# RWKV keys stage: the decay's small-rank products issued one key tile sooner than the rate's

## The chip, the cores and the metric

The kernel runs on one core of one Trainium2 chip. The metric is the time of one execution on the device in microseconds (us); several executions are timed and the median is given. One more execution is recorded by the hardware profiler, and all rows shown come from such a record. The engines are TensorE (PE in the rows; its weight loads are PEld), VectorE (DVE), ScalarE (ACT), GpSimd (POOL) and SyncE (SP), whose queue issues nearly all DMA transfers here.

## What is computed

The program is one inference step of a two-layer trunk on 1104 token rows: 8 sample sequences of 8 tokens, then a prompt of 16 + 1024. Layer 0 is a gated DeltaNet mixer, layer 1 an RWKV-7 mixer. Only the projections at the start of layer 1 matter here:

```python
xs = xn[None] + xx[None] * mu[:, None, None, :]             # six token-shifted mixes of the input
rkvz = jnp.einsum('sbtd,sde->sbte', xs[:4], w_rkvz)         # four 1024 x 1024 projections
r, k, v, z = rkvz[0], rkvz[1], rkvz[2], rkvz[3]
w = -jax.nn.softplus(-(w0 + jnp.tanh(xs[4] @ w1) @ w2)) - 0.5     # decay: rank 64
a = jax.nn.sigmoid(a0 + (xs[5] @ a1) @ a2)                        # rate: rank 64
kk = l2norm((k * k_k).reshape(B, T, H, N))
k = k * (1.0 + (a - 1.0) * k_a)
decay = jnp.exp(-jnp.exp(w))
```

The decay does not use the keys. The second form of the keys, `k * (1 + (a - 1) * k_a)`, needs keys and rate of the same columns.

## The kernel before, in words

All activations lie transposed: 128 features on the partitions, tokens along the free dimension, in three segments of 384, 384 and 336 tokens (`SEGS`). A 1024-wide result is made of 8 tiles of 128 features; in the keys projection they are called key tiles 0 to 7. A float32 product is made of three matmuls on rounded halves (high times high, high times low, low times high), so one segment of a key tile takes 8 x 3 = 24 matmuls and a whole key tile 72.

The keys stage is `keys_decay_rate` (L1425). It first prepares `w2`, the second small-rank matrices of decay and rate, split into `lw2h` and `lw2l`. The first small-rank products have been made before by `lora_first`; their results lie in `hh` (for the decay) and `hl` (for the rate), each in a high and a low half. Then it loops over the key tiles k:

- `projected(1, k, ...)` (keys): 72 matmuls into three of four PSUM buffers with the tag `d`. For k = 0 and 7 one segment after the other, otherwise the three segments side by side.
- For each segment: an ACT instruction scales the keys by `k_k` into a buffer `kev` (three buffers), which SP writes to DRAM (`kd`); DVE copies the keys into a buffer `key` (six buffers, so two tiles' worth). For k = 7 ACT does the copy.
- `lora_second(0, k, ...)` (decay of tile k): for each segment two matmuls into one of two PSUM buffers with the tag `f` (shown as `flora`), then `dst_w`: an ACT sigmoid into a buffer `ev` (three buffers, shared with the rate), a DVE scan along the tokens (L1456) into a buffer `ev2` (three, shared too; the rows call both `ev`), and a DMA to `csd` (L1457). For the last segment POOL first clears the end of the `ev` buffer (L1453).
- `lora_second(1, k, ...)` (rate of tile k): the same two matmuls, then `dst_a`: an ACT sigmoid, a DMA to `ad` (L1463), a DVE multiply-add (L1465), a DVE product with the kept keys (L1466), and a DMA to `k2d` (L1467), after which the `key` buffer is free.

"Product" below means the two matmuls of one segment of one tile of decay or rate; there are 8 x 3 of the decay and as many of the rate, 48 in all. They are called w0 to w7 and a0 to a7 by their key tile.

Two callbacks put work of the next stage between. `between(k)` (for k = 2, 3, 4) and `behind(s)` (only for k = 7: after each key segment, and once as `behind(3)` after the decay) mix the inputs of the receptance projection `r` (rows `mixs`, and the halves written to `xa`, `xc`) and load its first weights (`wraw`, split into `whi` by ACT and `wlo` by POOL, three buffers each). After key tile 3, six DMAs write 48 columns of zeros (`zpad`, L1488) behind the newest write of `k2d`.

What runs first on an engine is not written out by hand in this stage. A planner in the compiler walks through the program with its own estimate of every duration; on each engine it takes, of the instructions that it holds to be ready, the one that stands earliest in the program, and this fixes a static order for each engine. Each engine then executes its order strictly in sequence. So the order in which the source issues the work is a priority, not an order. From the projections `r`, `v`, `z` on, the order on PE is written out by hand.

Of the kernel before, what the change touches and what calls it, by code (L numbers as in the profile page):

```python
# [36 lines left out]
class Builder:  # L37
# [8 lines left out]
    def t(self, pool, shape, tag, bufs=1, dt=F32):  # L46
        self.uid += 1
        return pool.tile(shape, dt, name=f"{tag}_{self.uid}", tag=tag, bufs=bufs)
# [1376 lines left out]
    def keys_decay_rate(self, x, hh, hl, between, behind):  # L1425

        nc, t, i, col = self.nc, self.t, self.i, self.pcol
        with self.tc.tile_pool(name="lora", bufs=1, reuse_waits="tile") as pool:
            z = t(pool, [128, 8, 48], "zpad")
            nc.gpsimd.memset(z, 0.0)  # L1430
            omka = t(pool, [128, 8], "omka")
            nc.vector.tensor_scalar(omka, col["rwkv_k_a"], -1.0, 1.0, op0=ALU.mult, op1=ALU.add)
            sm = t(pool, [128, 384], "sm0")
            sm1 = t(pool, [128, 384], "sm1")
            self.scan_mask(sm, True)
            self.scan_mask(sm1, False)

            wr = t(pool, [128, 2, D], "lw2")
            for q in (0, 64):
                nc.sync.dma_start(wr[q:q + 64, 0], i["rwkv_w2"][0])  # L1440
                nc.sync.dma_start(wr[q:q + 64, 1], i["rwkv_a2"][0])
            w2 = t(pool, [128, 2, D], "lw2h", dt=F32R), t(pool, [128, 2, D], "lw2l", dt=F32R)
            nc.scalar.copy(w2[0], wr)

            for u, q in ((0, slice(0, 64)), (1, slice(64, 128))):
                nc.vector.tensor_tensor(w2[1][q, u], wr[q, u], w2[0][q, u].bitcast(F32), op=ALU.subtract)
                nc.gpsimd.memset(w2[1][64 - q.start:128 - q.start, u].bitcast(F32), 0.0)

            def dst_w(k, s, p):
                c0, n = SEGS[s]  # L1450
                f = t(self.ev, [128, 384], "ev", 3)
                if s == 2:
                    nc.gpsimd.memset(f[:, n:384], 0.0)  # L1453
                self.act(f[:, 0:n], p[:, 0:n], AF.Sigmoid, bias=col["rwkv_w0"][:, k:k + 1])
                g = t(pool, [128, 384], "ev2", 3)
                nc.vector.tensor_tensor_scan(g, sm if s == 0 else sm1, f, 0.0, op0=ALU.mult, op1=ALU.add)  # L1456
                nc.sync.dma_start(self.csd[k][:, c0:c0 + 384], g)  # L1457

            def dst_a(k, s, p):
                c0, n = SEGS[s]  # L1460
                f = t(self.ev, [128, 384], "ev", 3)
                self.act(f[:, 0:n], p[:, 0:n], AF.Sigmoid, bias=col["rwkv_a0"][:, k:k + 1])
                nc.sync.dma_start(self.ad[k][:, c0:c0 + n], f[:, 0:n])  # L1463
                g, kf = t(pool, [128, 384], "ev2", 3), keys.pop(0)
                nc.vector.tensor_scalar(g[:, 0:n], f[:, 0:n], col["rwkv_k_a"][:, k:k + 1], omka[:, k:k + 1], op0=ALU.mult, op1=ALU.add)  # L1465
                nc.vector.tensor_tensor(kf[:, 0:n], g[:, 0:n], kf[:, 0:n], op=ALU.mult)  # L1466
                self.newest = nc.sync.dma_start(self.k2d[k][:, c0:c0 + n], kf[:, 0:n]).ins  # L1467

            keys = []
            for k in range(8):  # L1470
                for s, ((c0, n), p) in enumerate(zip(SEGS, self.projected(1, k, x, k in (0, 7)))):
                    f = t(pool, [128, 384], "kev", 3)
                    scaled = self.act(f[:, 0:n], p[:, 0:n], AF.Identity, scale=col["rwkv_k_k"][:, k:k + 1]).ins
                    nc.sync.dma_start(self.kd[k][:, c0:c0 + n], f[:, 0:n])
                    keys.append(t(pool, [128, 384], "key", 6))
                    (nc.scalar.copy if k in (7,) else nc.vector.tensor_copy)(keys[-1][:, 0:n], p[:, 0:n])
                    if k == 7:
                        behind(s)
                self.lora_second(0, k, hh, w2, dst_w)
                if k == 7:  # L1480
                    behind(3)
                self.lora_second(1, k, hl, w2, dst_a)
                with self.tc.issue_after(scaled):
                    between(k)
                if k == 3:
                    with self.tc.issue_after(self.newest):
                        for d in (self.ad, self.rd, self.vd, self.zd, self.kd, self.k2d):
                            nc.sync.dma_start(d[:, :, NT:1152].rearrange("k p n -> p k n"), z)  # L1488
# [1065 lines left out]
```

## Time and profile before

| what | value |
|---|---|
| median of 3 runs | 2175.77 us (2173.61 to 2179.67) |
| profiled execution: own time | 2173.21 us |
| profiled execution: span of the core | 2171.5 us |
| mean granted TensorE clock | 0.982 |
| PE busy | 2046.2 us, 94% of the span |
| DVE busy | 1583.4 us, 73% |
| ACT busy | 1283.1 us, 59% |
| POOL busy | 834.9 us, 38% |

The span runs from the first to the last recorded instruction; the profiled execution's own time is 1.7 us longer, and lies 2.56 us under the median of the runs. Shares over the whole span hide the stages: the keys stage fills about 1290 to 1406 us of the span, and the projection `r` follows it.

### The profile page before, as it was taken

What the parts mean: (1) busy time and instruction counts of PE and PEld (TensorE: products, weight loads), DVE (VectorE), ACT (ScalarE), POOL (GpSimd) and SP (SyncE); (2) the same over time, 40 slices, a digit from 0 to 9 for tenths busy, and PEclk for the clock granted to TensorE, in tenths of its full rate; (3) what the DMA queues carried; (4) which work ended last, traced back from release to release, by engine and by line L of the source; (5) the groups of instructions that cost most, each with busy time, mean ns of one, the idle gap of its engine ahead of it and who ended that gap; (6) DMA issues with size and microseconds to landing.
All of it is one profiled execution on the core that took longest, in us unless ns stands there. A gap on an engine that the chain in (4) does not pass through costs nothing. (4 is left out here: it accounts for less than half of the span.)

```text
span 2171.5 us, 54811 instructions
## 1 busy us (share of the span) xinstructions
PE 2046.2 (94%) x20418; PEld 1905.8 (88%) x20418; DVE 1583.4 (73%) x4212; ACT 1283.1 (59%) x3750; POOL 834.9 (38%) x1136
## 2 busy tenths in 40 slices
PE   6969899999999999999999999889899999999997
PEld 5959899999999999998899999889798988888876
DVE  6968879698888979795334676757979557767755
ACT  4536565656565665656533365664747446677774
POOL 3523334334343333334231352344524254444444
PEclk9979999999999999999999999999999999999999
DMA  3424343424333333335345115655555486677754
GB/s 120 122 58 105 77 108 90 118 79 107 90 97 106 106 97 104 97 102 159 106 129 135 63 54 191 220 160 174 169 180 158 117 224 175 188 234 225 228 178 139
DMA packets 430724, 292.52 MB, mean 135 GB/s; under 512 B 147337, under 2 KB 413050, under 8 KB 430458
## 3 DMA queue, kind: packets, MB, share of 16 engines
q1 hardware_dynamic: 430458, 289.02, 46.2%
q8 instruction: 161, 2.64, 0.5%
q14 instruction: 105, 0.86, 0.1%
HBM read 197.55 MB, written 91.37 MB: 133 GB/s over the span
## 5 line engine op out<-in xcount | busy, mean ns | idle before, releaser
L91 POOL TENSOR_TENSOR wlo<-wraw,whi 128x512 fp32r<-128x512 f32 (+1 forms) x246 | 331.1, 1348 | 465.6 <-ACT whi L87 413.9
L77 PE MATMUL d<-xc,whi 128*128 128x384 f32 (+2 forms) x1006 | 279.5, 337 | 4.8 <-ACT whi L87 4.1
L526 DVE SCALAR_TENSOR_TENSOR cvy<-raw,cw,cvy 128x408 f32<-128x408 f32 (+2 forms) x288 | 199.0, 692 | 17.1 <-ACT cvy L63 15.7
L87 ACT CAST whi<-wraw 128x512 fp32r<-128x512 f32 (+1 forms) x246 | 149.8, 611 | 88.1 <-PE d L77 51.2
L77 PEld LDWEIGHTS d<-xc,whi 128*128 128x128 f32 (+1 forms) x1006 | 183.4, 189 | 7.8 <-ACT whi L87 4.8
L77 PE MATMUL d<-xc,wlo 128*128 128x384 f32 (+3 forms) x476 | 157.7, 340 | 2.7 <-POOL wlo L91 2.7
L77 PE MATMUL dz<-xc,whi 128*128 128x384 f32 (+1 forms) x480 | 153.9, 338 | 0.0
L77 PE MATMUL dv<-xc,whi 128*128 128x384 f32 (+1 forms) x480 | 152.4, 337 | 0.0
L77 PE MATMUL d<-xa,whi 128*128 128x384 f32 (+3 forms) x450 | 142.1, 340 | 4.5 <-ACT whi L87 1.7
L63 ACT ACTIVATE o<-rA,gcol 128x128 f32<-128x128 f32 x128 | 42.0, 366 | 116.9 <-DVE S L905 116.7
L573 DVE TENSOR_TENSOR invtmp<-invA,invT 72x31 f32<-72x31 f32 (+15 forms) x248 | 102.2, 412 | 3.2
L77 PE MATMUL dv<-xa,whi 128*128 128x384 f32 (+1 forms) x288 | 99.1, 344 | 0.0
L77 PE MATMUL dz<-xa,whi 128*128 128x384 f32 (+1 forms) x288 | 98.6, 342 | 0.0
L575 DVE TENSOR_TENSOR invT<-invT,invtmp 72x31 f32<-72x31 f32 (+15 forms) x248 | 95.0, 383 | 3.3
L77 PEld LDWEIGHTS d<-xc,wlo 128*128 128x128 f32 (+1 forms) x476 | 89.3, 189 | 6.8 <-POOL wlo L91 3.6
L77 PEld LDWEIGHTS dz<-xc,whi 128*128 128x128 f32 x480 | 89.4, 189 | 4.6 <-issue 4.5
L77 PEld LDWEIGHTS d<-xa,whi 128*128 128x128 f32 (+1 forms) x450 | 83.9, 189 | 8.2 <-issue 3.7
L77 PEld LDWEIGHTS dv<-xc,whi 128*128 128x128 f32 x480 | 89.2, 188 | 1.4 <-issue 1.4
L77 PE MATMUL d<-xa,wlo 128*128 128x384 f32 (+3 forms) x252 | 84.9, 337 | 1.4 <-POOL wlo L91 1.4
L77 PE MATMUL dk<-xc,whi 128*128 128x384 f32 (+1 forms) x240 | 79.3, 349 | 0.0
L77 PE MATMUL dq<-xc,whi 128*128 128x384 f32 (+1 forms) x240 | 77.0, 338 | 0.0
L1335 DVE SCALAR_TENSOR_TENSOR mixs<-xb,pcol,mixs 128x320 f32<-128x320 f32 (+2 forms) x96 | 68.6, 725 | 5.9 <-ACT mixs L63 5.6
(542 smaller groups left out, 6801.0 us busy)
## 6 DMA issues: line engine op xcount, KB each, us to landing
wraw<-in_gdn_w_in SPq DMA_DIRECT2D x96, 256.0 KB
wraw<-in_rwkv_w_rkvz SPq DMA_DIRECT2D x80, 256.0 KB
Sb<-in_state_gdn SPq DMA_DIRECT2D x64, 256.0 KB
sldcak<-cakd SPq DMA_DIRECT2D x24, 576.0 KB
wraw<-in_rwkv_w_o SPq DMA_DIRECT2D x42, 256.0 KB
E<-drow SPq DMA_DIRECT2D x24, 384.0 KB
attn<-drow SPq DMA_DIRECT2D x24, 384.0 KB
wraw<-in_gdn_w_out SPq DMA_DIRECT2D x36, 256.0 KB
```

The source lines that it names most:

```text
L63: return self.nc.scalar.activation(out, in_, func, bias=bias, scale=scale, **kw)
L77: self.nc.tensor.matmul(out, lhsT, rhs, start=start, stop=stop)
L87: nc.scalar.copy(hi, x)
L91: e.tensor_tensor(lo, x, hi.bitcast(F32), op=ALU.subtract)
L526: nc.vector.scalar_tensor_tensor(y[0][:, 0:wd], raw[:, k:k + wd], cw[k], y[0][:, 0:wd], op0=ALU.mult, op1=ALU.add)
L573: nc.vector.tensor_tensor(tmp, A[:, j, j + 1:32].unsqueeze(2).broadcast_to([nb, n, m]), Tv[:, j, 0:m].unsqueeze(1).broadcast_to([nb, n, m] ...
L575: nc.vector.tensor_tensor(Tv[:, j + 1:32, 0:m], Tv[:, j + 1:32, 0:m], tmp, op=ALU.subtract)
L1335: nc.vector.scalar_tensor_tensor(x[:, f:], xb[:, 8 + a + f:8 + b], mu, x[:, f:], op0=ALU.mult, op1=ALU.add)
```

## The change

The second small-rank products of the decay are issued in the source one key tile sooner, and those of the rate stay. Behind the keys of tile 0 stand now w0, w1 and a0; behind the keys of tile k (1 to 6) stand w(k+1) and a(k); behind the keys of tile 7 stands only a7. The order of the products in the source was w0 a0 w1 a1 w2 a2 ... w7 a7 and is now w0 w1 a0 w2 a1 w3 a2 ... w7 a6 a7. Nothing is added or removed.

```diff
                     if k == 7:
                         behind(s)
-                self.lora_second(0, k, hh, w2, dst_w)
+                for q in {0: (0, 1), 7: ()}.get(k, (k + 1,)):
+                    self.lora_second(0, q, hh, w2, dst_w)
                 if k == 7:
                     behind(3)
                 self.lora_second(1, k, hl, w2, dst_a)
```

## Prediction

> **What bounds the kernel now.** I read the page first, then the windows of the keys stage, then PE, DVE and ACT in order of time at its end.
>
> ```profile
> span 2171.5 us, 54811 instructions
> PE 2046.2 (94%) x20418; PEld 1905.8 (88%) x20418; DVE 1583.4 (73%) x4212; ACT 1283.1 (59%) x3750; POOL 834.9 (38%) x1136
> ```
>
> PE is the bound of the whole. So the change can only be worth what PE loses near it. The windows (length, then busy time of PE, PEld, DVE, ACT and POOL with instruction counts, granted clock, DMA share, GB/s) show where that is:
>
> ```profile
> 1360.00:1380.00 20.00, 20.00 (x121) 20.00 (x120) 10.92 (x20) 9.00 (x17) 3.57 (x6) 1.00 0.94 274
> 1380.00:1395.00 15.00, 13.67 (x82) 13.35 (x80) 13.94 (x24) 14.27 (x34) 6.12 (x7) 1.00 0.50 178
> 1395.00:1406.00 11.00, 6.86 (x18) 4.33 (x19) 11.00 (x18) 7.69 (x18) 4.41 (x5) 0.61 0.68 237
> 1406.00:1419.00 13.00, 12.76 (x72) 12.48 (x70) 12.03 (x20) 8.26 (x20) 6.19 (x9) 0.94 0.57 194
> 1419.00:1432.00 13.00, 7.49 (x28) 6.78 (x29) 9.38 (x14) 11.07 (x24) 6.93 (x9) 0.74 0.31 108
> ```
>
> Up to 1380 PE is full and DVE half idle (9.1 of 20 us). From 1380 to 1419 it is the other way round: DVE is busy 36.97 of 39 us, and PE gets only 18 matmuls into 1395 to 1406, at a granted clock of 0.61. The small-rank products, by tile and then in order of time on PE:
>
> ```profile
> L77 PE MATMUL flora<-xa,lw2h x48: 310/338/690, 1303.5 to 1404.8; 128*128 128x384 f32 x32, 128*128 128x336 f32 x16
> 1303.46 0.51 PE L77 MATMUL flora<-xa,lw2h 128*128 128x384 f32 x2
> ...
> 1338.63 0.34 PE L77 MATMUL flora<-xa,lw2h 128*128 128x384 f32 x1
> ...
> 1347.20 0.34 PE L77 MATMUL flora<-xa,lw2h 128*128 128x384 f32 x1
> 1347.72 0.34 PE L77 MATMUL flora<-xa,lw2h 128*128 128x384 f32 x1
> 1351.58 0.32 PE L77 MATMUL flora<-xa,lw2h 128*128 128x336 f32 x1
> ...
> 1389.99 0.34 PE L77 MATMUL flora<-xa,lw2h 128*128 128x384 f32 x1
> ...
> 1392.85 0.31 PE L77 MATMUL flora<-xa,lw2h 128*128 128x336 f32 x1
> ...
> 1396.34 0.45 PE L77 MATMUL flora<-xa,lw2h 128*128 128x384 f32 x1 [2.67 <-ACT ev L63]
> ...
> 1398.19 0.69 PE L77 MATMUL flora<-xa,lw2h 128*128 128x384 f32 x1 [0.80 <-ACT ev L63]
> 1399.63 0.69 PE L77 MATMUL flora<-xa,lw2h 128*128 128x384 f32 x1 [0.42 <-ACT ev L63]
> 1402.22 0.65 PE L77 MATMUL flora<-xa,lw2h 128*128 128x336 f32 x1 [1.58 <-ACT ev L63]
> ...
> 1404.78 0.65 PE L77 MATMUL flora<-xa,lw2h 128*128 128x336 f32 x1
> 1405.50 0.52 PE L77 MATMUL d<-xa,whi 128*128 128x384 f32 x1
> 1421.07 0.33 PE L77 MATMUL d<-xc,whi 128*128 128x384 f32 x1
> 1425.53 0.69 PE L77 MATMUL d<-xc,whi 128*128 128x384 f32 x1 [4.13 <-ACT whi L87]
> ```
>
> The products go in pairs, one pair for each turn of the two `f` buffers: the 1st and 2nd start at 1303.46, the 37th at 1389.99, so 18 pairs take 86.5 us, 4.8 us each. At this pace the decays and rates run a key tile behind the keys: the row at 1392.85 is the 39th product (w6's last segment, as 39 = 6 x 6 + 3), and the last keys matmul has just ended. Ten products are left, and they are the tail: 12.65 us from 1392.85 to the first matmul of `r` at 1405.50, with 2.67 + 0.80 + 0.42 + 1.58 = 5.47 us in which PE waits for ACT to free an `f` buffer.
>
> **The change part by part.** *Work.* The same 48 products with the same matmuls, sigmoids, scans, POOL clears and DMAs: 0 us.
>
> *Place in the stream.* Counting through the new order, w(k+1) and a(k) change places: a(k) was products 6k+4 to 6k+6 and is 6k+7 to 6k+9; only w0 and a7 keep theirs. The pace is set by the two `f` buffers, and an evacuation of either kind frees its buffer by the same ACT sigmoid, so I expect the same 38 products before 1392.85 and ten behind. What differs is who the ten are: now the end of w6, a6, w7, a7; then the end of a5 (a5 is 37 to 39), w7, a6, a7. So nothing is taken out of the tail; its scans become rates.
>
> ```profile
> L1456 DVE TENSOR_TENSOR_SCAN ev<-sm,ev 128x384 f32<-128x384 f32 x24 | 24.7, 1048 | 11.8 <-ACT ev L63 11.7
> L1466 DVE TENSOR_TENSOR key<-ev,key 128x384 f32<-128x384 f32 (+1 forms) x24 | 13.2, 568 | 0.2
> L1465 DVE TENSOR_SCALAR ev<-ev,pcol,omka 128x384 f32<-128x384 f32 (+1 forms) x24 | 12.9, 558 | 5.0 <-DMA cakd<-ev 3.1 <-ACT ev L63 1.8
> ```
>
> *DVE in the tail.* From product 37 on DVE now does 6 scans and 6 rates; then 3 scans and 9 rates. A rate costs 0.558 + 0.568 = 1.13 us, a scan 1.05: 3 x 0.08 = +0.2 us, on the engine that is full there.
>
> *ACT's waits in the tail.* ACT also waits itself:
>
> ```profile
> 1399.04 0.54 ACT L63 ACTIVATE ev<-flora,pcol 128x336 f32<-128x336 f32 x1 [0.90 <-DVE ev L1456]
> ...
> 1401.58 0.58 ACT L63 ACTIVATE ev<-flora,pcol 128x384 f32<-128x384 f32 x1 [0.79 <-DMA cakd<-ev]
> ...
> 1407.58 0.54 ACT L63 ACTIVATE ev<-flora,pcol 128x336 f32<-128x336 f32 x1 [0.24 <-DVE ev L1456]
> ```
>
> These are sigmoids that wait for an `ev` buffer, twice for a scan (1.14 us). With a6 and a7 back to back no scan stands between them: between 0 and -1.1 us; I take -1.1, since the waits have their rows and the DMA wait of 0.79 stays as it is.
>
> *Key buffers.* a(k) frees the `key` buffers that key tile k+2 wants, and comes three products, 1.5 pairs, 7.2 us later.
>
> ```profile
> 1341.52 0.58 ACT L63 ACTIVATE kev<-d,pcol 128x384 f32<-128x384 f32 x1 [0.71 <-ACT xa L87]
> ...
> 1350.93 1.01 ACT L63 ACTIVATE kev<-d,pcol 128x384 f32<-128x384 f32 x2
> ```
>
> ```profile
> 1343.98 0.56 DVE L1476 COPY key<-d 128x384 f32<-128x384 f32 x1 [2.03 <-DMA cakd<-key]
> ...
> 1371.41 0.48 DVE L1465 TENSOR_SCALAR ev<-ev,pcol,omka 128x384 f32<-128x384 f32 x1 [3.13 <-DMA cakd<-ev]
> ...
> 1376.61 0.56 DVE L1476 COPY key<-d 128x384 f32<-128x384 f32 x1 [2.47 <-DMA cakd<-key]
> ```
>
> Key tile 4's first segment is done at 1341.5 and copied at 1343.98, when the DMA of a2's first product has freed a buffer; that is product 16, at 1338.63. So 5.4 us pass from a product to a free `key` buffer. With a2 in places 19 to 21 (1347.20, 1347.72, 1351.58) the copies of tile 4 come at 1352.6, 1353.1 and 1357.0, against keys done at 1341.5 and 1350.9, and their `d` buffers are held so long. At 1350.9 PE turns to key tile 5 with one `d` buffer free and the second from 1352.6. One segment alone is 24 matmuls; at 13.67 us for 82 (windows) that is 4.0 us, so it covers PE until 1354.9. Cost 0, with a cover of 2.3 us; it holds as long as the path from product to free buffer does not grow from 5.4 to over 7.7 us. If the cover is gone, that is the slower rival. On DVE nothing else is delayed unless the planner puts a copy ahead of work that is ready: the copy at 1376.61 held DVE for 2.47 us in that way.
>
> *Queues.* SP sees `csd` of w(k+1) ahead of `ad` and `k2d` of a(k); in the tail the last scan's DMA stands ahead of a6's, as now w6's does. POOL's clear (L1453) for w7 comes three products sooner. Both 0.
>
> *Zero columns.* They follow a3's last `k2d`, so they also move 7.2 us.
>
> ```profile
> L1488 SPq DMA_DIRECT2D cakd<-zpad x3: 426/1181/1895, 1361.9 to 1366.4; - x3
> ```
>
> The DMA share is 0.94 in 1360 to 1380, and the two DVE waits for DMA above (3.13 and 2.47 us, at 1368.3 to 1371.4 and 1374.1 to 1376.6) lie in that stretch, where DVE has time. Moved by 7.2 they would lie at 1375.5 to 1378.6 and 1381.3 to 1383.8: the second inside the full stretch. Between 0 and +2.5 us; I take +1, because DVE still has 1.06 idle us of 15 in 1380 to 1395.
>
> Sum: 0 + 0.2 - 1.1 + 0 + 1 = +0.1 us on the profiled execution's 2173.2 (span 2171.5 and 1.7 around it), which lies 2.56 under the median; on the median 2175.77 + 0.1 = 2175.9.
>
> **Weighed against a page.** POOL and DVE stretch each other in the tail:
>
> ```profile
> 1393.15 2.03 DVE L1456 TENSOR_TENSOR_SCAN ev<-sm,ev 128x384 f32<-128x384 f32 x1
> 1393.03 1.33 POOL L91 TENSOR_TENSOR wlo<-wraw,whi 128x512 fp32r<-128x512 f32 x1 [1.00 <-ACT whi L87]
> ```
>
> This scan took 2.03 us beside a POOL split, against the mean of 1.05. The Trainium skill, SBUF — State Buffer, section "SBUF: two separate sides", says that VectorE instructions with two SBUF inputs and GpSimd's instructions that read SBUF take one port pair in turn, and the loser stands still. By that rule the scan should gain the time for which POOL holds the port, and the trace agrees.
>
> **The rivals.** *The products get ahead* (faster). If the later copies make the planner hold back keys matmuls, PE takes small-rank products in their place, and fewer than ten are left at the end of the keys. Eight moved ahead take 8 x 1.09 = 8.7 us of DVE work (the mean of scan and rate) from the full stretch into the idle 9.1 us before 1380: 2167.1. Against it: two `f` buffers pace the products whatever they are. `r` cannot gain more than DVE gives, since its inputs are mixed there.
>
> *The key buffers run out* (slower). If landings lengthen the 5.4 us beyond 7.7, PE stands at the start of key tiles 3, 5 and 7 (those whose predecessor has its first segment early, as tile 4 at 1341.5). A wait like the one at 1376.61, 2.5 us, at each: +7.5, or 2183.3. For it: DMA is at 0.94 at 1360 to 1380. Against it: the waits for `key` do not stop PE now (20.00 of 20 us), and only the last of the three places is near that stretch.
>
> *Port collisions fall otherwise.* The scan above lost 1.0 us; four such shifts in the tail either way are 4: 2172 or 2180. The page's rule gives this case, and the mechanism is that of the two rows.
>
> *Nothing moves.* The planner could keep places so that only names change; the wait of 4.13 us at 1425.53, behind ACT, swallows what is left: 2175.8.
>
> **How the numbers follow.** A measurement of this kernel tells about 0.3% (6.5 us) from no change. Forecast 0.44 (own range 2171 to 2181); ahead 0.22; buffers run out 0.18; port 0.08; nothing moves 0.08. Of ahead 0.03, of running out 0.02 and of the port 0.07 stay within 0.3%; 0.01 of the port is slower. Faster 0.19, same 0.44 + 0.03 + 0.02 + 0.07 + 0.08 = 0.64, slower 0.16 + 0.01 = 0.17. The range 2166 to 2185 takes in both outer rivals' times with a little beyond, and leaves out about 0.1 on either side.
>
> **What would show it.** Right: the product rows still in pairs some 4.8 us apart, about ten of 48 behind the last keys matmul, the first matmul of `r` within 2 us of 1405.5, `key` copies waiting more often for DMA than twice, PE still full in 1310 to 1390, the zeros at about 1369 to 1374. Wrong: PE gaps before key tiles 3, 5 or 7; six products or fewer in the tail; a wait for `whi` at the second tile of `r` much longer or shorter than 4.13; or a shift of several us that first appears behind 1432, where the change touches nothing.

## The result and the profile after

The changed kernel is slower by a little more than this kernel's measurement can tell: 2188.96 us, the median of 7 runs (2181.5 to 2191.21), against 2177.14 for 7 runs of the kernel before (2173.61 to 2181.7); the ratio on record is 1.0035, 95% interval 1.002 to 1.005. (The quotient of the two medians is 1.0054; the repeat speaks for the smaller figure.) Measured again beside the experiments (`again`): 1.0031, 1.002 to 1.0043. On the median of before that the prediction started from, a ratio of 1.0035 gives 2183.4 us. So the likeliest case (no change, 2175.9) did not come, and the time is that of the rival in which the key buffers run out (2183.3). It lies near the upper end of the stated range of 2166 to 2185, and outside the likeliest case's own range of 2171 to 2181.

The windows of the keys stage of the kernel after (length, busy time of PE, PEld, DVE, ACT, POOL, granted clock, DMA share, GB/s):

```profile
1360.00:1380.00 20.00, 18.29 (x110) 17.86 (x109) 13.49 (x25) 9.42 (x20) 4.75 (x5) 1.00 0.57 186
1380.00:1395.00 15.00, 13.69 (x81) 13.41 (x81) 10.88 (x19) 9.53 (x21) 4.88 (x5) 1.00 0.94 264
1395.00:1410.00 15.00, 9.66 (x48) 7.90 (x47) 14.40 (x22) 12.13 (x28) 6.40 (x6) 0.84 0.47 159
1410.00:1423.00 13.00, 11.46 (x45) 10.02 (x46) 12.40 (x21) 7.68 (x17) 5.67 (x4) 0.66 0.57 209
```

PE was full to 1390 before; it now has gaps in 1360 to 1380 and again in 1380 to 1395. In order of time on PE, the gaps and the tail:

```profile
1375.93 0.62 PE L77 MATMUL d<-xc,whi 128*128 128x384 f32 x2 [1.71 <-DVE key L1476]
...
1392.27 0.44 PE L77 MATMUL d<-xc,whi 128*128 128x384 f32 x1 [1.31 <-DVE key L1476]
...
1397.05 0.34 PE L77 MATMUL flora<-xa,lw2h 128*128 128x384 f32 x1
...
1400.97 0.32 PE L77 MATMUL flora<-xa,lw2h 128*128 128x336 f32 x1
...
1404.94 0.61 PE L77 MATMUL flora<-xa,lw2h 128*128 128x384 f32 x1 [3.15 <-ACT ev L63]
...
1408.85 0.69 PE L77 MATMUL flora<-xa,lw2h 128*128 128x384 f32 x1 [2.01 <-ACT ev L63]
1410.07 0.69 PE L77 MATMUL flora<-xa,lw2h 128*128 128x384 f32 x1 [0.20 <-ACT ev L63]
1412.47 0.65 PE L77 MATMUL flora<-xa,lw2h 128*128 128x336 f32 x1 [1.40 <-ACT ev L63]
...
1415.04 0.65 PE L77 MATMUL flora<-xa,lw2h 128*128 128x336 f32 x1
...
1415.77 0.52 PE L77 MATMUL d<-xa,whi 128*128 128x384 f32 x1
```

Twice PE waits for a DVE key copy, 3.02 us together. The 37th product stands at 1397.05 and the 39th at 1400.97, so again ten products are behind the last keys matmul. The last row is the first matmul of `r`. The view of the waits in the same stage (us in all, times, longest), first the kernel before, then after:

```profile
DVE key L1476 <- DMA cakd<-key: 4.5, 2, 2.5
```

```profile
DVE key L1476 <- DMA cakd<-key: 19.1, 11, 4.4
...
PE d L77 <- DVE key L1476: 3.0, 2, 1.7
...
ACT whi L87 <- DMA cakd<-zpad: 2.4, 1, 2.4
```

DVE's waits for a key write to land have grown fourfold, and PE's waits for the copies are new.

The spans differ by 16.0 us, more than the runs do. The order on PE is the same up to key tile 1, and yet the stage begins 4.4 us later in this execution; over all profiled executions of this study it begins between 1288.1 and 1295.7. So I compare the length of the stage: from the first keys matmul to the ACT copy of the first segment of the fourth tile of `r`. Before (first two rows) and after:

```profile
1290.10 0.33 PE L77 MATMUL d<-xh,whi 128*128 128x384 f32 x1
...
1459.76 0.46 ACT L2354 COPY ev<-d 128x384 f32<-128x384 f32 x1
```

```profile
1294.50 0.33 PE L77 MATMUL d<-xh,whi 128*128 128x384 f32 x1
...
1470.80 0.48 ACT L2355 COPY ev<-d 128x384 f32<-128x384 f32 x1 [0.69 <-PE d L77]
```

169.66 us before, 176.30 after: +6.6, and +6.8 in `again`. The ratio of 1.0035 is 7.6 us, so the loss lies in the stage. Of the 6.6 us, 5.9 are there by the last product (1404.78 - 1290.10 = 114.68 before, 1415.04 - 1294.50 = 120.54 after). They come in three parts: 3.7 us up to the 39th product, 2.15 us from there to the first matmul of `r` (12.65 before, 14.80 after), and 0.8 us behind it.

### The profile page after: what moved, and what is told of

It is laid out like the page before. It is cut to its first block, busy times and chain, and to the rows that moved or that the text cites. A ratio compares the mean times of both kernels' runs of the same rounds, so it can differ in the third digit from the quotient of the medians.

```text
span 2187.5 us, 54807 instructions
## 1 busy us (share of the span) xinstructions
PE 2055.4 (94%) x20418; PEld 1911.8 (87%) x20418; DVE 1583.3 (72%) x4212; ACT 1284.5 (59%) x3750; POOL 836.9 (38%) x1136
## 5 line engine op out<-in xcount | busy, mean ns | idle before, releaser
L63 ACT ACTIVATE mixs<-xb,omu 128x64 f32<-128x64 f32 (+3 forms) x128 | 61.5, 520 | 19.8 <-DVE xc L91 7.8
```

The lines of the kernel that those rows point to most:

```text
L63: return self.nc.scalar.activation(out, in_, func, bias=bias, scale=scale, **kw)
```

## The experiments

Theory A: the rates come three products later, the `key` buffers are freed too late, DVE and then PE stand for them. Rival B: the zero columns fall into a worse place. Rival C: the new order of the last products. "Stage" below is the length just defined, from one profile each (it repeats well: 176.30 and 176.46 for the changed kernel, and 169.66, 169.79 and 169.67 for `before`, `old_keys8` and `only_w7`, whose times do not differ); "waits" is the time for which DVE's key copies wait for key writes.

| run | order, and what differs | ratio to before (95%) | stage, us | waits, us (times) |
|---|---|---|---|---|
| before | old | | 169.66 | 4.5 (2) |
| `again` | new | 1.0031 (1.002 to 1.0043) | 176.46 | 15.9 (7) |
| `new_keys8` | new, 8 key buffers | 1.0003 (0.999 to 1.0017) | 171.70 | 5.2 (3) |
| `old_keys8` | old, 8 key buffers | 1.0006 (0.9995 to 1.0017) | 169.79 | none |
| `old_keys5` | old, 5 key buffers | 1.0015 (1.0002 to 1.0028) | 172.41 | 12.7 (8) |
| `new_zeros2` | new, zeros behind a2 | 1.0017 (1.0002 to 1.0031) | 173.44 | 13.2 (9) |
| `old_zeros5` | old, zeros behind a5 | 1.0009 (0.9994 to 1.0024) | 172.92 | 7.7 (3) |
| `new_keys8_zeros2` | new, both | 1.0003 (0.999 to 1.0015) | 171.32 | 2.4 (2) |
| `only_w7` | old, w7 ahead of a6 | 0.9991 (0.9977 to 1.0006) | 169.67 | 7.2 (3) |
| `all_but_w7` | new, w7 behind a6 | 1.0028 (1.0013 to 1.0042) | 175.91 | 18.7 (8) |
| `old_psum4` | old, 4 product buffers | 0.9986 (0.9972 to 1.0) | 165.55 | none |
| `new_psum4` | new, 4 product buffers | 0.9994 (0.9982 to 1.0007) | 163.91 | none |
| `w7_psum4` | `only_w7`, 4 product buffers | 1.0004 (0.9988 to 1.0019) | 167.82 | none |

**The change once more.**

> The changed kernel once more, beside the others. All theories: 7 to 12 us over the kernel before (2177); DVE's key copies wait some 19 us for the key writes to land, PE waits some 3 us for those copies, the zero columns are issued about 12 us later in the stage than before.

Nearly as expected: 0.31% is 6.8 us, the copies wait 15.9 us, PE waits 2.5 us for them, and the zero columns come 11.7 us later in the stage than before.

**More key buffers, new order.**

```diff
-                    keys.append(t(pool, [128, 384], "key", 6))
+                    keys.append(t(pool, [128, 384], "key", 8))
```

> The changed order with 8 key buffers in place of 6. Theory A (the key buffers are freed three products later than the copies want them, and the queue of DVE and then PE stands for it): DVE's waits of key copies for DMA fall from 19.1 us to under 5, PE's waits for key copies from 3.0 to 0, and the time comes back to within 3 us of the kernel before (2177). Rival B (the six writes of zero columns, which now fall 12 us later, into the end of the stage): stays 7 to 12 us slower, since the zeros keep their place behind a3. Rival C (the order of the last products alone, a6 and a7 back to back): stays slower by 7 to 12 us, with the waits for key copies gone.

Theory A held but for 0.2 us of the waits (5.2 us, expected under 5); B and C did not. The windows and the waits of `new_keys8`:

```profile
1360.00:1380.00 20.00, 20.00 (x121) 20.00 (x121) 13.16 (x22) 9.20 (x19) 4.65 (x6) 1.00 0.60 184
1380.00:1395.00 15.00, 15.00 (x90) 15.00 (x89) 11.54 (x21) 11.51 (x26) 4.33 (x5) 1.00 0.88 261
```

```profile
DVE key L1476 <- DMA cakd<-key: 5.2, 3, 2.7
```

PE has no gap up to 1395 and the time is that of before, though order and zeros stand where the change put them. 4.8 of the 6.8 us of `again` are gone from the stage; 2.0 are not.

**More key buffers, old order (control).** The same edit on the kernel before.

> Control: the order of before with 8 key buffers. Theory A (8 buffers cured the changed order because copies there waited for key writes): the old order has little of this wait (4.5 us in two copies, none of it reaching PE), so the time stays within 3 us of the kernel before (2179). Rival: 8 buffers are worth some 6 us in any order, and then this kernel is about 6 us faster than before and the cure of the changed order shows nothing on its cause.

Theory A held: the buffers are worth nothing where nobody waits for them, so `new_keys8` is a cure and no separate gain.

**Fewer key buffers, old order.** `"key", 5` on the kernel before.

> The order of before with 5 key buffers in place of 6: each key copy needs the buffer of one rate product later, which in the old order is one to four places in the stream of products, so a part of the lateness of the changed order without its order. Theory A: DVE's waits of key copies for DMA rise from 4.5 us to 10 or more, and the time by 3 to 10 us. Rivals B and C: no change (under 2 us), as zeros and the last products keep their places.

The old order with late buffers behaves like a weaker form of the new one:

```profile
DVE key L1476 <- DMA cakd<-key: 12.7, 8, 2.6
```

The ratio, 1.0015, is at the low end of what A expected (3.3 us), and the interval almost reaches no change; the stage is 2.75 us longer. PE waits for no key copy in this run: the loss is in the tail, 14.9 us from the 39th product to `r` in place of 12.65. So late copies can cost time without PE standing for them.

**The zero columns sooner, new order.**

```diff
-                if k == 3:
+                if k == 2:
                     with self.tc.issue_after(self.newest):
```

> The changed order with the zero columns written behind a2 in place of a3, so that they fall a tile sooner, where DVE has idle time. Theory A: the waits for key copies stay 12 us or more and the kernel stays at least 5 us slower than before. Rival B: the waits behind 1370 us go, and the time is within 3 us of the kernel before. Rival C: stays 7 to 12 us slower.

Between A and B: the waits stay, but the ratio is only 3.7 us over before, less than A's 5, and 3.0 of the 6.8 us of `again` are gone from the stage:

```profile
DVE key L1476 <- DMA cakd<-key: 13.2, 9, 4.1
...
PE d L77 <- DVE key L1476: 0.9, 1, 0.9
```

These 3.0 us are not won in the keys, though. The first matmul of `r` lies 123.03 us into this stage, later than in `again` (121.05) and in `before` (115.40):

```profile
1417.57 0.52 PE L77 MATMUL d<-xa,whi 128*128 128x384 f32 x1
```

The gain comes behind it, in the first tiles of `r`, where PE waits 3.2 us against 6.5 in `again`. So this run does not show how the place of the zeros acts.

**The zero columns later, old order.** `if k == 5:` on the kernel before.

> The order of before with the zero columns behind a5 in place of a3, later than in the changed kernel. It prices the zeros' place alone. Theory A: up to 2 us, since the old order's copies wait little. Rival B: 4 us or more slower than before, DVE or ACT waiting for landings behind the zeros.

In the stage the zeros cost 3.3 us here, more than A's bound of 2 and less than B's 4; the ratio does not tell it from no change. The zeros begin 99.8 us into this stage, later than in the changed kernel (84.1), so this is not the price of the changed kernel's place; and PE waits for no key copy here either.

**Both edits, new order.**

> The changed order with 8 key buffers and the zero columns behind a2. Theory A with the zeros as a smaller second cause: at or up to 4 us under the changed order with 8 buffers alone (2181.7 in the last set, 0.03% over the kernel before), so within 3 us of the kernel before. Theory A alone: the same as with 8 buffers alone. Rival C (the last products' order costs by itself): still 2 us behind the kernel before in the stage, from its first keys matmul to the fourth tile of r.

With enough key buffers the zeros' place is worth 0.4 us in the stage, so the 3.0 us above are no price that the zeros have by themselves; the two shares (4.8 and 3.0 us of 6.8) overlap and are not to be added. The stage is still 1.7 us longer than before, near the 2 us that rival C expected here; the next two runs test C itself.

**Only the end of the change, and all but the end.**

```diff
-                for q in {0: (0, 1), 7: ()}.get(k, (k + 1,)):
+                for q in {6: (6, 7), 7: ()}.get(k, (k,)):            # only_w7
+                for q in {0: (0, 1), 6: ()}.get(k, (k + 1 if k < 7 else k,)):   # all_but_w7
```

> Only the end of the change: w7 comes ahead of a6, all else in the order of before. Theory A: only a6 is late, and no key tile is left that wants its buffers (tile 8 does not exist), so no copy waits longer and the time stays within 2 us of the kernel before. Rival C (order of the last products): 5 us or more slower.

> The change without its end: w1 to w6 come a key tile sooner, w7 stays between a6 and a7. Theory A (key buffers of tiles 2 to 7 freed three products late): as slow as the changed kernel, 0.2 to 0.5% over before, DVE's waits of key copies for DMA 12 us or more, and 5 to 8 us more than before from the first keys matmul to the fourth tile of r. Rival C (order of the last products): no slower than before by more than 2 us.

The times of both are as theory A expected, and against C. One detail is not: in `only_w7` the copies wait 7.2 us against 4.5, where A expected no longer waits; the stage does not show it. Moving w7 costs nothing; moving w1 to w6, behind each of which a rate that still has key tiles waiting for it is put back, brings nearly the whole loss, 6.25 us of the stage:

```profile
DVE key L1476 <- DMA cakd<-key: 18.7, 8, 4.6
...
PE d L77 <- DVE key L1476: 2.5, 2, 1.3
```

**Four PSUM buffers for the products.**

```diff
-            p = self.ps("f", 2, "lora")
+            p = self.ps("fg"[(3 * x + s) % 2], 2, "lora")
```

> The order of before with the products' PSUM buffers doubled (two under the tag f, two more under a new tag, taken in turn). It asks whether two buffers set the pace of one pair of products per 4.8 us, as the prediction held. If they do: four products go per turn, the decays and rates catch up with the keys, six or fewer products are left behind the last keys matmul instead of ten, and the kernel is 3 to 9 us faster than before. If the pace is set elsewhere (the three ev buffers, or the key writes): still about ten left and no change within 3 us.

The pace was indeed set by two buffers: the first 18 pairs take 4.26 us each in place of 4.81, six products are left behind the last keys matmul, the stage is 4.1 us shorter, and the ratio of 0.9986 touches no change.

> The changed order with four PSUM buffers for the products. With four, the old order left six products behind the last keys matmul and was 0.14% faster. Theory A: the rates now come soon enough after their keys, though still three places later than in the old order, so the copies' waits fall below 8 us, PE does not wait for them, and the kernel is within 3 us of the old order with four buffers (2172.6 beside 2174.4). If the changed order costs for a reason that has nothing to do with when the key buffers come free, it is 6 us or more over that one.

Theory A again: with the pace raised, the new order costs nothing. The products by tile in `new_psum4`:

```profile
L77 PE MATMUL flora<-xa,lw2h x24: 315/338/343, 1304.2 to 1396.4; 128*128 128x384 f32 x16, 128*128 128x336 f32 x8
L77 PE MATMUL glora<-xa,lw2h x24: 312/336/343, 1304.4 to 1396.7; 128*128 128x384 f32 x16, 128*128 128x336 f32 x8
```

Three products are left behind the last keys matmul, none of the 48 takes over 343 ns, and the stage is the shortest of all, 5.75 us under before. The whole kernel is not faster to match (0.9994, at best 0.9982); one profile each cannot tell where it is given back.

> Both parts that did not cost: four PSUM buffers for the products and only w7 ahead of a6. No theory of the cause hangs on it; as the effects were 0.9986 and 0.9991 apart, I expect 0.996 to 0.9995 of the kernel before, about six products left behind the last keys matmul.

No gain: 1.0004, outside the expected range, and three products are left, not six. None of the versions tried is clearly faster than the kernel before.

## Why the prediction was right or wrong

The stated range held because it had been drawn around the rivals' times, not because the likeliest case was right: its forecast of no change missed by 7.5 us on the scale of the prediction, and what came is the slower rival, to which it gave 0.18. The step by which it set that rival aside is the one that failed. Of the signs that it named, the pairs and the ten products came out as forecast; PE's gaps in the keys and the first matmul of `r` (121.27 us into the stage, where 115.40 was before and 2 us were allowed) speak against it.

*Work: right.* PE issues 20418 matmuls and DVE 4212 instructions in both.

*Place in the stream: right.* Pairs as before (18 pairs from 1307.86 to 1397.05, 4.96 us each against 4.81), ten products left; the pace is set by the product buffers, as `old_psum4` shows. So the faster rival, products that get ahead, had no ground in this kernel. The products got ahead only when the buffers were doubled, and then the time fell by some 3 us (0.9986), not by the rival's 8.7.

*Key buffers: the step that failed.* It counted 5.4 us from a rate's product to a free buffer and a cover of 2.3 us, hence 0 up to 7.7 us, and named the case that would undo it: the planner puts a copy ahead of work that is ready. That is what it did. One turn of it after the change, from the rows of PE, DVE, SP and ACT around a3 (its first product is the 25th, its third the 27th):

```profile
1366.11 0.42 PE L77 MATMUL flora<-xa,lw2h 128*128 128x384 f32 x1
...
1370.60 0.32 PE L77 MATMUL flora<-xa,lw2h 128*128 128x336 f32 x1
```

```profile
1371.11 0.54 ACT L63 ACTIVATE ev<-flora,pcol 128x336 f32<-128x336 f32 x1 [0.52 <-PE flora L77]
```

```profile
1367.34 1.87 DVE L1456 TENSOR_TENSOR_SCAN ev<-sm,ev 128x384 f32<-128x384 f32 x1
...
1369.90 1.01 DVE L1466 TENSOR_TENSOR key<-ev,key 128x384 f32<-128x384 f32 x2
1375.32 1.15 DVE L1476 COPY key<-d 128x384 f32<-128x384 f32 x2 [4.41 <-DMA cakd<-key]
1376.39 0.45 DVE L1465 TENSOR_SCALAR ev<-ev,pcol,omka 128x336 f32<-128x336 f32 x1
...
1380.69 0.51 DVE L1476 COPY key<-d 128x336 f32<-128x336 f32 x1 [2.59 <-DMA cakd<-key]
```

```profile
1369.65 1.46 SPq L205 DMA_DIRECT2D wraw<-in_rwkv_w_rkvz  x1
1371.21 0.93 SPq L1463 DMA_DIRECT2D cakd<-ev  x2
1372.23 0.94 SPq L1467 DMA_DIRECT2D cakd<-key  x2
```

a3's first product is at 1366.11, its DVE product begins at 1369.90 (the row holds two and ends at 1370.91), its DMA is issued at 1372.23 behind a weight load and two others on SP, and the copies of key tile 5 start at 1375.32: 9.2 us, not 5.4, and over the 7.7. The same points before, for a2's first product at 1338.63, whose buffer is copied into at 1343.98, are these rows of DVE and SP:

```profile
1341.40 0.55 DVE L1466 TENSOR_TENSOR key<-ev,key 128x384 f32<-128x384 f32 x1
```

```profile
1341.98 0.32 SPq L1467 DMA_DIRECT2D cakd<-key  x1
```

Of the 3.9 us by which the path grew, 1.0 lies ahead of the DVE product (the scan there took 1.87 us beside a POOL split, where scans alone take 0.95), 1.75 between its start and the issue on SP, and 1.1 between the issue and the copy.

While DVE stands 4.41 us for this, a3's third rate, whose sigmoid began at 1371.11, lies behind the copies and runs at 1376.39. So the wait lengthens the next path and feeds itself: from a3's third product (1370.60) to the copy that gets its buffer (1380.69) it is 10.1 us. PE gets its `d` buffer at 1375.93. I had taken the path as a constant of the old order.

The rival was right in that the path outgrew 7.7 us, though the landings that it named gave only 1.1 of the 3.9 us. That its size fits the time (+7.5; measured 6.6 to 6.8 in the stage) is luck, since its places do not: PE stood twice and at tiles 6 and 7, for 3.0 us, not three times for 7.5; the rest came as a longer tail (2.15 us) and in smaller parts around it (1.5 us).

*Queues: wrong.* I set the order on SP at 0. The rows above show a key write waiting there for 1.3 us behind other issues; before, it was issued as soon as it was ready (1341.95 and 1341.98). From the stage's start to 1416 us SP stood 32.4 us for scans of DVE after the change, and 19.2 us before.

*Zero columns: moved too little; their price stays open.* I moved them 7.2 us and took +1. They follow a3's last key write, which is itself late:

```profile
1378.58 0.44 SPq L1489 DMA_DIRECT2D cakd<-zpad  x1
```

That is 84.1 us into the stage against 71.8: 12.3 later. PE's first wait (1375.93) lies before them, so they did not begin the loss. What their place costs is not settled: 3.0 us of the stage in the new order, won behind the first matmul of `r`; 3.3 in the old order at a still later place; 0.4 with eight key buffers.

*ACT's waits in the tail: right, but the 1.1 us did not reach PE.* No sigmoid of the tail waits long for a scan any more; two short waits for a landing are left:

```profile
1409.47 0.54 ACT L63 ACTIVATE ev<-flora,pcol 128x336 f32<-128x336 f32 x1 [0.27 <-DMA cakd<-ev]
...
1414.41 0.58 ACT L63 ACTIVATE ev<-flora,pcol 128x384 f32<-128x384 f32 x1 [0.34 <-DMA cakd<-ev]
```

But PE's waits for ACT in the tail rose from 5.47 to 3.15 + 2.01 + 0.20 + 1.40 = 6.76 us. ACT now makes key tile 7's copies there (the last at 1411.50, before at 1395.40), but that they are the cause is not shown: the same waits are 6.4 us in `new_keys8` and in `old_keys8`, where these copies are not late.

*DVE's +0.2 and the port rival* cannot be priced apart by these runs; that POOL lengthens scans is seen (last section). *Left open:* the 2.0 us by which `new_keys8` is still longer than before in the stage. Of them 1.85 are there by its last product; but `old_keys8` and `only_w7` too have their last product 1.0 and 0.9 us later than before, and lose nothing by the end of the stage. w7's place is not the cause (`only_w7`), a5 among the last ten products may be, which was not tried.

## What to carry to other kernels

Before work is moved ahead of other work in a stream whose pace is limited, ask what the other work releases: here the rates freed the key buffers, the decays freed nothing that was scarce. A slack read from the old trace (5.4 us from work to free buffer) is a property of the old order: where an engine that keeps its order stands in the wait, as DVE did for 4.41 us, it delays the very work that would end it, and the path has to be followed again with that queue standing. And before an order is tuned, look at what sets the pace: doubling the two product buffers shortened the stage by 4.1 us in the old order and made the new one harmless, though neither kernel was clearly faster as a whole.

## What the runs showed of the hardware

TensorE slowed in a stretch whose waits are all short: in the tail after the change no wait is over 3.15 us, and yet the small matmul that takes 338 ns in the median takes 0.69 us at 1408.85, 1410.07 and 1414.12, at a granted clock of 0.66 in 1410 to 1423. Before, it took as long at 1398.19, behind waits of 2.67 and 0.80 us. In `new_psum4`, where PE does not wait for ACT at these products, none of the 48 took over 343 ns.

A DVE scan was lengthened by a two-input instruction of POOL only where POOL had begun first. In the 14 traces of this study, among the rows of a single scan between 1300 and 1425 us, 24 began while such a POOL instruction ran: 22 of them took 1.18 to 2.05 us, the longer the more of it was left, and the other two 0.94 and 0.96 us, where it had begun 0.04 us before or had 0.09 us left. In another 24 POOL began during the scan, and they took 0.94 to 0.96 us; 71 that met no such POOL instruction took 0.92 to 0.96.

A stage's start in the record moved by up to 7.6 us between executions with the same work ahead of it, so the length of a stage told 3 us where the span did not.
